# Attention scores drained two PSUM banks at a time, fewer value products in plain fp32, and the operand buffers of the out-projection placed earlier

## The chip, the cores and the metric

The kernel runs on one core of one Trainium2 chip. The metric is the device time of one execution in microseconds (us); the median of the runs is compared. A core has a matrix engine (PE, whose weight loads are listed as PEld), a vector engine (DVE), a scalar engine (ACT), a general engine (POOL) and a queue engine that issues transfers (SP). PE writes its results into PSUM, 8 banks of 512 fp32 columns for each of 128 partitions; the other engines read them from there.

## The reference

One block of a diffusion backbone over 2048 latent tokens of width 1024 with 256 context tokens: modulated norm, one input projection, gated linear attention (GLA, 4 heads) and differential softmax attention (4 heads, width 128) side by side, one output projection, and a modulated SwiGLU FFN. The part that the change is about:

```python
def diff_attend(q, k_all, v_all, lam):            # 2048 queries, 2304 keys, 2 maps of width 64
    s = jnp.einsum('bhqcd,bhkcd->bhcqk', qb, k_all) * (DIFF_DH ** -0.5)
    p = jax.nn.softmax(s, axis=-1)
    a = p[:, :, 0] - lam * p[:, :, 1]
    return jnp.einsum('bhqk,bhkd->bhqd', a, v_all)
...
mix = jnp.concatenate([gla_merge(...), diff_merge(...)], axis=-1) @ w_out[l]
x = x + gt1 * mix
```

Everything is fp32. Most products are made of three fp32r matmuls on operands split into a high and a low part; a plain fp32 matmul takes two passes on PE.

## The kernel before

The program has six stages one behind the other: projections (0 to some 400 us), the GLA scan (to 875), attention (scores from 875.6 to 1481.5, its last value products to 1516), the output projection (to 1751), and the two FFN products.

**Attention.** There are 16 blocks: 4 heads by 4 groups of 512 queries. A block has 4 query tiles of 128; each tile has two maps, and each map's scores over 2304 keys are made in 5 chunks (CH: four of 512 columns and one of 256), so a block has 8 maps and 40 chunks. For a chunk, two matmuls (L775, L776; the high and the low part of the queries) fill one PSUM bank `s`; one DVE instruction (L777) copies the bank into the row buffer p0 or p1 and takes its maximum into a column of `mx`. After the fifth chunk DVE reduces `mx` to `nm` (L781) and ACT makes the exponentials of the whole row with their sum (L783). Four chunks after the second map, `combine` weights the second map (r and cf, L799 and L801; p1 times cf in two halves, L807) and POOL adds the halves to p0 (L83).

**Value products.** The stream `av_stream` runs 12 chunks behind. A block has 18 key tiles. For each the step is: four transposes of p0 into a PSUM tile `t` (L820); a copy out of it; and, two steps later (LOOK), the product with that key tile's values. Key tiles with kt % 6 in VFP, (0, 3) before, stay fp32: one ACT copy `at` (L823) and one fp32 matmul (L843). The others are split: ACT writes the high part `ah` (L89), DVE the rest `al` (L86), and three fp32r matmuls follow (L92 to L94). In a block, a step follows the chunks 1, 4, 6, 8, 10, 12, 15, 17, 19, 21, 24, 26, 28, 30, 32, 35, 37 and 39 (counted from 0). At a block's end ACT copies the result (`ot`, L848), PE transposes it (L860), ACT copies it (`on`, L862), and SP stores it to `md` (L864).

**PSUM.** The score pool ps_s has NS = 4 tiles of one bank, ps_t 3, ps_o 1: all 8 banks.

**Order.** The order on PE is the order of the code (manual_schedule with MS = PE). On DVE, ACT, POOL and SP a scheduler orders by priorities, and each engine then runs its list strictly in that order.

**Values.** Stage 1 stores the values either as fp32 (key tiles in VF) or as high and low parts; `load_v` (L735 to L750) loads them per head and third of the keys.

**Output projection.** For each token tile `prep` loads `md` into mx (L976), takes the square sums on ACT (L985, which writes its unused squares into mh), the deviation (L990) and its inverse (L992), scales (L995), transposes (L1002) and makes mh and ml, the two parts of the operand (L1004 to L1007); `main` multiplies by w_out (L1010). The pools ph (mh, ml), htp and wp are opened one behind the other (L914 to L916), so their order sets which addresses of the finished attention they reuse.

Of the kernel before, what the change touches and what calls it, by code (L numbers as in the profile page):

```python
# [11 lines left out]
F32 = mybir.dt.float32  # L12
F32R = mybir.dt.float32r
AF = mybir.ActivationFunctionType
ALU = mybir.AluOpType
AX = mybir.AxisListType
PSUM = bass.MemoryType.PSUM
DRAM = bass.MemoryType.DRAM

P = 128  # L20
# [12 lines left out]
NS, NTB, NO = 4, 3, 1  # L33
# [6 lines left out]
CD, LAG, LOOK = 4, 12, 2  # L40
MS = {mybir.EngineType.PE}
BKL = (3, 6, 9, 12)
PB, VFP = 6, (0, 3)
CSPLIT = ((2, 0, 1152), (2, 1152, 2304))
WPOOL = (0,)
VF = tuple(t for t in range(NK // P) if t % 6 in VFP)
# [5 lines left out]
def dit_block(ctx: ExitStack, tc: tile.TileContext, x, c, cx, c_ctx, w_mod, b_mod, norm1_g, w_in, gate_up,  # L52
              gate_bias, gla_g, qn_g, kn_g, lam_q, lam_k, diff_g, w_out, norm2_g, w_fi, w_fo,
              cosf, sinf, lmask, out, dbg=None):
    nc = tc.nc
    V, S, T, G = nc.vector, nc.scalar, nc.tensor, nc.gpsimd
# [115 lines left out]
    with ExitStack() as st:  # L172
# [3 lines left out]
        st1 = st.enter_context(ExitStack())  # L176
# [12 lines left out]
        for t in range(2):  # L189
            xt = wk.tile([P, D], F32, name="xt", tag="xt")  # L190
# [514 lines left out]
    with ExitStack() as st:  # L705
        sm = st.enter_context(tc.tile_pool(name="s3m", bufs=6, reuse_waits="tile"))
# [4 lines left out]
        qp = st.enter_context(tc.tile_pool(name="s3q", bufs=2, reuse_waits="tile"))  # L711
        kp_ = st.enter_context(tc.tile_pool(name="s3k", bufs=3, reuse_waits="tile"))
        pb = st.enter_context(tc.tile_pool(name="s3pb", bufs=PB, reuse_waits="tile"))
        ps_s = st.enter_context(tc.tile_pool(name="s3ps", bufs=NS, space=PSUM, reuse_waits="tile"))
        ps_t = st.enter_context(tc.tile_pool(name="s3pt", bufs=NTB, space=PSUM, reuse_waits="tile"))
        ps_o = st.enter_context(tc.tile_pool(name="s3po", bufs=NO, space=PSUM, reuse_waits="tile"))
        NKT = NK // P
        CH = [(0, 512), (512, 512), (1024, 512), (1536, 512), (2048, 256)]
# [42 lines left out]
        def score_stream():  # L761
            later, ring = [], iter(range(64))
            for bi, (h, qb, i0, nq) in enumerate(blocks):
                as_[bi] = []
                for i in range(i0, i0 + nq):
                    qd = qs_[h, qb, i // 2]
                    qc = slice(i % 2 * P, (i % 2 + 1) * P)
                    pr = [(pa if next(ring) % (4 + PB) < 4 else pb).tile([P, NK], F32, name="p0", tag="p0"), sp.tile([P, NK], F32, name="p1", tag="p1")]
                    as_[bi].append(pr[0])
                    ls = []  # L770
                    for c_ in range(2):
                        mx = sm.tile([P, 5], F32, name="mx", tag="mx")
                        for j, (o0, n) in enumerate(CH):
                            ps = ps_s.tile([P, 512], F32, name="s", tag="s")
                            T.matmul(ps[:, 0:n], qd[0][c_][:, qc], ks_[h, c_][:, o0:o0 + n], start=True, stop=False)  # L775
                            T.matmul(ps[:, 0:n], qd[1][c_][:, qc], ks_[h, c_][:, o0:o0 + n], start=False, stop=True)  # L776
                            V.tensor_scalar(out=pr[c_][:, o0:o0 + n], in0=ps[:, 0:n], scalar1=1.0, scalar2=-3.0e38,  # L777
                                            op0=ALU.mult, op1=ALU.max, accum_out=mx[:, j:j + 1])
                            if j == len(CH) - 1:
                                nm = sm.tile([P, 1], F32, name="nm", tag="nm")  # L780
                                V.tensor_reduce(out=nm, in_=mx, axis=AX.X, op=ALU.max, negate=True)  # L781
                                l = l0all[:, qb * 4 + i, h:h + 1] if c_ == 0 else sm.tile([P, 1], F32, name="l1", tag="l1")
                                S.activation(pr[c_], pr[c_], AF.Exp, bias=nm, accum_out=l)  # L783
                                ls.append(l)
                                if c_ == 1:
                                    later.append([CD, combine(pr, ls, bi == len(blocks) - 1 and i >= i0 + nq - 2)])
                            for e in list(later):
                                e[0] -= 1
                                if e[0] < 0:
                                    e[1]()  # L790
                                    later.remove(e)
                            yield
            for e in later:
                e[1]()
# [72 lines left out]
        due, n = [], 0  # L867
# [26 lines left out]
    with ExitStack() as st:  # L894
# [16 lines left out]
        st1 = st.enter_context(ExitStack())  # L911
        xlp = rsk.enter_context(tc.tile_pool(name="s4xl", bufs=1, side="right", reuse_waits="tile"))
        gp = st1.enter_context(tc.tile_pool(name="s4gt", bufs=1, reuse_waits="tile"))
        htp = st1.enter_context(tc.tile_pool(name="s4ht", bufs=2, reuse_waits="tile"))  # L914
        wp = st1.enter_context(tc.tile_pool(name="s4w", bufs=1, reuse_waits="tile"))
        ph = st1.enter_context(tc.tile_pool(name="s4h", bufs=2, reuse_waits="tile"))  # L916
        ps_gm = st1.enter_context(tc.tile_pool(name="s4gm", bufs=1, space=PSUM, reuse_waits="tile"))
        ps_tp = st1.enter_context(tc.tile_pool(name="s4tp", bufs=3, space=PSUM, reuse_waits="tile"))
        ps_mm = st1.enter_context(tc.tile_pool(name="s4mm", bufs=4, space=PSUM, reuse_waits="tile"))
# [9 lines left out]
        state = {}  # L929
        wo = {k: tuple(wp.tile([P, D], F32R, name=f"wo{u}_{k}") for u in "hl") for k in ORD1}  # L930
        for n, k in enumerate(ORD0):
            pool, tag = {3: (xnp, "xn"), 2: (xnp, "xn"), 1: (ph, "mh"), 0: (ph, "ml")}.get(k, (xp, "xt"))
            w = pool.tile([P, D], F32, name="wr", tag=tag)
            load(w, w_out[0, k * P:(k + 1) * P, :])
            with tc.high_priority(offset=tc.cur_priority - marks[3 + 2 * n]):
                split(*wo[k], w)
# [316 lines left out]
        with tc.manual_schedule(engines=MS):  # L1253
# [6 lines left out]
            for m, (n, i) in enumerate(flat):  # L1260
# [13 lines left out]
                ps = product(n, i)  # L1274
# [104 lines left out]
```

## Time and profile before

| what | value |
|---|---|
| runs | 3092.88, 3094.99 and 3092.88 us, median 3092.88 |
| profiled execution | 3094.64 us, of which the span of the trace is 3092.9 |
| busy share over the span | PE 98%, PEld 80%, DVE 71%, ACT 46%, POOL 15% |
| granted clock of PE, mean | 0.992 of full speed |
| attention scores | 875.6 to 1481.5 us, a block each 38.2 us |

Read the shares with care: 98% of PE is a mean over stages, and the 71% of DVE too. In the attention stage both are nearly full, and there the rows below were read: how busy each engine is in stretches of 38 us (one block), who waits for whom, and the distance from one instruction's start to the next one's, which is what an instruction costs on a full engine (its own duration includes an overlap with its neighbour).

### The profile page before, as it was taken

The numbers are of one execution on the slowest core, as the hardware profiler recorded it, in microseconds if no ns is written. First come the engines' busy times: TensorE is split into PE (matmuls) and PEld (weight loads), VectorE is DVE, ScalarE is ACT, GpSimd is POOL, SyncE is SP. The second block draws the span as 40 slices with busy tenths as digits, with TensorE's granted clock in tenths as the row PEclk, the third lists the DMA queues.
The fourth block names the chain that finished last, engine by engine and source line by source line (L and its number), as shares of the span: only waits on it lengthen the run. The fifth ranks groups of instructions, "written<-read, shape, count | busy, mean of one in ns | idle before, by whom it ended". The sixth has DMA issues, their size and how long they took to land.

```text
span 3092.9 us, 41887 instructions
## 1 busy us (share of the span) xinstructions
PE 3016.1 (98%) x15124; PEld 2483.7 (80%) x15124; DVE 2203.8 (71%) x4788; ACT 1423.5 (46%) x2259; POOL 463.8 (15%) x290
## 2 busy tenths in 40 slices
PE   7999999999989999999999999999999999999999
PEld 4888888888867777777787788888788888888887
DVE  6887768888889999999787776666766666324232
ACT  5333366666657777777644433333433333113111
POOL 2111100000036555555111000000000000000000
PEclk9999999999999999999999999999999999999999
DMA  8876511121151313121445442222322225445342
GB/s 312 280 237 224 192 66 63 66 93 65 49 154 34 91 34 93 35 76 35 143 164 163 158 136 82 82 85 69 88 82 86 82 86 179 149 136 180 130 135 90
DMA packets 319121, 363.46 MB, mean 118 GB/s; under 512 B 25409, under 2 KB 256258, under 8 KB 312258
## 3 DMA queue, kind: packets, MB, share of 16 engines
q1 hardware_dynamic: 316322, 351.35, 36.2%
q0 software_dynamic: 2304, 8.39, 0.7%
q8 instruction: 119, 1.95, 0.3%
q10 hardware_dynamic: 288, 1.05, 0.1%
q14 instruction: 88, 0.72, 0.1%
HBM read 249.96 MB, written 110.76 MB: 117 GB/s over the span
## 4 chain that ended last, share of the span: by engine, by line
PE 63%; DVE 4%; issue 2%; DMA 1%; ACT 1%; POOL 1%; DVEq 0%; SPq 0%; ACTq 0%; POOLq 0%
PE p L93 9%; PE p L92 9%; PE p L94 9%; PE o L93 6%; PE o L94 6%; PE o L92 6%; PE s L775 4%; PE s L776 4%; PE t L820 4%; PE o L843 3%; PE mm L92 1%; PE mm L93 1%; PE mm L94 1%; POOL p L83 0%; DMA wo<-in_w_ffn_out 0%
## 5 line engine op out<-in xcount | busy, mean ns | idle before, releaser
L83 POOL TENSOR_TENSOR p<-p,p 128x1152 f32<-128x1152 f32 x124 | 354.8, 2882 | 283.5 <-DVE p L807 175.8
L777 DVE TENSOR_SCALAR_CACHE_REDUCE p<-s 128x512 f32<-128x512 f32 (+1 forms) x640 | 382.3, 632 | 13.2 <-PE s L776 9.2
L92 PE MATMUL mm<-wh,hh 128*128 128x512 f32 (+2 forms) x976 | 378.7, 388 | 0.0
L94 PE MATMUL mm<-wh,hl 128*128 128x512 f32 (+2 forms) x976 | 355.0, 364 | 1.1 <-DVE hl L86 1.1
L93 PE MATMUL mm<-wl,hh 128*128 128x512 f32 (+2 forms) x976 | 353.8, 363 | 0.0
L783 ACT ACTIVATE p<-p,nm 128x2304 f32<-128x2304 f32 x128 | 283.8, 2217 | 44.5 <-DVE nm L781 44.5
L775 PE MATMUL s<-k,qh 128*128 128x512 f32 (+1 forms) x640 | 276.4, 436 | 7.7 <-DVE p L777 6.9
L83 DVE TENSOR_TENSOR e<-p,e 128x512 f32<-128x512 f32 x220 | 152.1, 691 | 161.1 <-PE p L94 161.1
L92 PE MATMUL o<-wot,ah 128*128 128x512 f32 x682 | 265.4, 389 | 1.1 <-ACT wot L89 1.1
L93 PE MATMUL o<-wot,ah 128*128 128x512 f32 x682 | 265.4, 389 | 0.2 <-DVE wot L86 0.2
L94 PE MATMUL o<-wot,al 128*128 128x512 f32 x682 | 265.3, 389 | 0.0
L89 ACT ACTIVATE wh<-wi 128x512 fp32r<-128x512 f32 x172 | 108.4, 631 | 293.4 <-PE p L93 228.4
L776 PE MATMUL s<-k,ql 128*128 128x512 f32 (+1 forms) x640 | 235.6, 375 | 1.3 <-DMA ql<-ql 1.3
L89 ACT ACTIVATE ah<-ar 128x1408 fp32r<-128x1408 f32 x62 | 82.6, 1374 | 318.0 <-PE o L93 314.4
L94 PEld LDWEIGHTS mm<-wh,hl 128*128 128x128 f32 x976 | 184.8, 189 | 31.2 <-DVE hl L86 1.5
L92 PEld LDWEIGHTS mm<-wh,hh 128*128 128x128 f32 x976 | 185.9, 190 | 22.9 <-issue 0.7
L93 PEld LDWEIGHTS mm<-wl,hh 128*128 128x128 f32 x976 | 186.1, 191 | 21.4 <-issue 0.5
L86 DVE TENSOR_TENSOR al<-ar,ah 128x1408 fp32r<-128x1408 f32 x62 | 98.3, 1622 | 134.1 <-ACT ah L89 134.1
L89 ACT ACTIVATE wh<-s 128x512 fp32r<-128x512 f32 x128 | 80.9, 632 | 221.9 <-PE p L93 208.5
L820 PE MATMUL t<-ident,p 128*128 128x128 f32 x1152 | 173.3, 273 | 0.8 <-POOL p L83 0.8
L820 PEld LDWEIGHTS t<-ident,p 128*128 128x128 f32 x1152 | 141.5, 141 | 35.3 <-issue 3.7
L775 PEld LDWEIGHTS s<-k,qh 128*128 128x128 f32 x640 | 122.5, 191 | 57.9 <-DVE p L777 15.8
(317 smaller groups left out, 7135.9 us busy)
## 6 DMA issues: line engine op xcount, KB each, us to landing
ar<-act SPq DMA_DIRECT2D x64, 704.0 KB, 5.9
wi<-in_w_ffn_in SPq DMA_DIRECT2D x86, 512.0 KB, 5.0
act<-e SPq DMA_DIRECT2D x88, 256.0 KB, 2.6
wm<-in_w_mod SPq DMA_DIRECT2D x32, 512.0 KB, 5.0
xt<-in_x SPq DMA_DIRECT2D x30, 512.0 KB, 4.7
wr<-in_w_in SPq DMA_DIRECT2D x12, 1024.0 KB, 7.8
hdh<-hh SPq DMA_DIRECT2D x9, 1024.0 KB, 4.8
hdl<-hl SPq DMA_DIRECT2D x9, 1024.0 KB, 6.6
```

The costliest lines, as they stand in the source:

```text
L83: (eng or V).tensor_tensor(out=o, in0=a, in1=b, op=ALU.add)
L86: return (eng or V).tensor_tensor(out=o, in0=a, in1=b, op=ALU.subtract)
L89: return S.activation(hi, src, AF.Copy), sub(lo, src, f(hi))
L92: T.matmul(ps, a[0], b[0], start=start, stop=False, **how)
L93: T.matmul(ps, a[0], b[1], start=False, stop=False, **how)
L94: T.matmul(ps, a[1], b[0], start=False, stop=stop, **how)
L775: T.matmul(ps[:, 0:n], qd[0][c_][:, qc], ks_[h, c_][:, o0:o0 + n], start=True, stop=False)
L776: T.matmul(ps[:, 0:n], qd[1][c_][:, qc], ks_[h, c_][:, o0:o0 + n], start=False, stop=True)
L777: V.tensor_scalar(out=pr[c_][:, o0:o0 + n], in0=ps[:, 0:n], scalar1=1.0, scalar2=-3.0e38, op0=ALU.mult, op1=ALU.max, accum_out=mx[:, j:j + 1])
L783: S.activation(pr[c_], pr[c_], AF.Exp, bias=nm, accum_out=l)
L820: T.transpose(pt[:, i, :], as_[bi][i][:, kt * P:(kt + 1) * P], ident)
L843: T.matmul(po[:, 0:nq, :], v[0], at[0], start=kt == 0, stop=kt == NKT - 1)
```

## The change

1. The score pool has two tiles of two banks instead of four of one. Chunks 0 and 1 share a tile, chunks 2 and 3 too, chunk 4 has one alone. One DVE instruction drains a tile: 1024, 1024 and 256 columns per map, 3 instead of 5. A row's `mx` has 3 columns.
2. VFP is (0,): key tiles 0, 6 and 12 of a block stay fp32, and 3, 9 and 15 are split like the others. So 48 of the 96 fp32 steps become split ones. Stage 1 stores three key tiles more in two parts, and load_v's tiles hold 1, 5 and 5 key tiles instead of 2, 4 and 4.
3. The pool ph is opened ahead of htp and wp; two raw rows of w_out use the buffers of mx instead of mh and ml. At the new addresses mh lies over the buffers of the last `al`, `ot` and `on` of attention; ml and the weights move up.

```diff
-PB, VFP = 6, (0, 3)
+PB, VFP = 6, (0,)
...
-        ps_s = st.enter_context(tc.tile_pool(name="s3ps", bufs=NS, space=PSUM, reuse_waits="tile"))
+        ps_s = st.enter_context(tc.tile_pool(name="s3ps", bufs=NS // 2, space=PSUM, reuse_waits="tile"))
...
-                        mx = sm.tile([P, 5], F32, name="mx", tag="mx")
+                        mx = sm.tile([P, 3], F32, name="mx", tag="mx")
                         for j, (o0, n) in enumerate(CH):
-                            ps = ps_s.tile([P, 512], F32, name="s", tag="s")
+                            if j % 2 == 0:
+                                ps2 = ps_s.tile([P, 2, 512], F32, name="s", tag="s")
+                            ps = ps2[:, j % 2]
...
-                            V.tensor_scalar(out=pr[c_][:, o0:o0 + n], in0=ps[:, 0:n], scalar1=1.0, scalar2=-3.0e38,
-                                            op0=ALU.mult, op1=ALU.max, accum_out=mx[:, j:j + 1])
+                            if j % 2 or j == len(CH) - 1:
+                                a0 = j // 2 * 1024
+                                V.tensor_scalar(out=pr[c_][:, a0:o0 + n], in0=ps2.rearrange("p b n -> p (b n)")[:, 0:o0 + n - a0],
+                                                scalar1=1.0, scalar2=-3.0e38, op0=ALU.mult, op1=ALU.max,
+                                                accum_out=mx[:, j // 2:j // 2 + 1])
...
+        ph = st1.enter_context(tc.tile_pool(name="s4h", bufs=2, reuse_waits="tile"))
         htp = st1.enter_context(tc.tile_pool(name="s4ht", bufs=2, reuse_waits="tile"))
         wp = st1.enter_context(tc.tile_pool(name="s4w", bufs=1, reuse_waits="tile"))
-        ph = st1.enter_context(tc.tile_pool(name="s4h", bufs=2, reuse_waits="tile"))
...
-            pool, tag = {3: (xnp, "xn"), 2: (xnp, "xn"), 1: (ph, "mh"), 0: (ph, "ml")}.get(k, (xp, "xt"))
+            pool, tag = {3: (xnp, "xn"), 2: (xnp, "xn"), 1: (pp, "mx"), 0: (pp, "mx")}.get(k, (xp, "xt"))
```

**First place: PE at the border of two maps without a value step between them** (chunks 33 to 35 of a block; the numbers of the tiles `s` tell which tile a matmul fills). Before, PE runs from the end of a step into these rows:

```order
L94 MATMUL o_12522<-ah_12648,vl1_10931 128x512
L775 MATMUL s_12716<-k1_10676,qh0_12427 128x512
L776 MATMUL s_12716<-k1_10676,ql0_12429 128x512
L775 MATMUL s_12728<-k1_10676,qh0_12427 128x256
L776 MATMUL s_12728<-k1_10676,ql0_12429 128x256
L775 MATMUL s_12736<-k1_12262,qh1_12428 128x512
L776 MATMUL s_12736<-k1_12262,ql1_12430 128x512
L820 MATMUL t_12740<-ident_60,p0_11848 128x128
```

And of the changed kernel, at the same place:

```order
L94 MATMUL o_12344<-ah_12465,vl1_10822 128x512
L778 MATMUL s_12517<-k1_10578,qh0_12253 128x512
L779 MATMUL s_12517<-k1_10578,ql0_12255 128x512
L778 MATMUL s_12543<-k1_10578,qh0_12253 128x256
L779 MATMUL s_12543<-k1_10578,ql0_12255 128x256
L778 MATMUL s_12551<-k1_12096,qh1_12254 128x512
L779 MATMUL s_12551<-k1_12096,ql1_12256 128x512
L826 MATMUL t_12554<-ident_60,p0_11701 128x128
```

The order of the matmuls is the same; what moved is whose banks they fill. With two tiles in turn, s_12551 takes the banks of s_12517, the tile that PE filled last but one; before, s_12736 took the bank of the chunk four earlier.

**Second place: DVE at the same border.** Before, DVE has these rows:

```order
L86 TENSOR_TENSOR al_12694<-t_12688,ah_12693 128x512
L777 TENSOR_SCALAR p0_12669,mx_12671<-s_12698 128x512
L777 TENSOR_SCALAR p0_12669,mx_12671<-s_12702 128x512
L777 TENSOR_SCALAR p0_12669,mx_12671<-s_12716 128x512
L799 RECIPROCAL r1_12720<-l1_12667 128x1
L777 TENSOR_SCALAR p0_12669,mx_12671<-s_12728 128x256
L801 TENSOR_SCALAR cf_12722<-l0all_80,r1_12720,neglam_81 128x1
L781 TENSOR_REDUCE nm_12732<-mx_12671 128x1
L777 TENSOR_SCALAR p1_12670,mx_12735<-s_12736 128x512
L807 TENSOR_SCALAR p1_12558<-p1_12558,cf_12722 128x1152 x2
```

And of the changed kernel:

```order
L86 TENSOR_TENSOR al_12510<-t_12504,ah_12509 128x512
L782 TENSOR_SCALAR p0_12486,mx_12488<-s_12489 128x1024
L805 RECIPROCAL r1_12535<-l1_12484 128x1
L807 TENSOR_SCALAR cf_12537<-l0all_80,r1_12535,neglam_81 128x1
L813 TENSOR_SCALAR p1_12381<-p1_12381,cf_12537 128x1152
L86 TENSOR_TENSOR al_12526<-t_12520,ah_12525 128x512
L782 TENSOR_SCALAR p0_12486,mx_12488<-s_12517 128x1024
L813 TENSOR_SCALAR p1_12381<-p1_12381,cf_12537 128x1152
L782 TENSOR_SCALAR p0_12486,mx_12488<-s_12543 128x256
L787 TENSOR_REDUCE nm_12547<-mx_12488 128x1
```

Three drains of 512 became one and a half of 1024; one half of the combination and the `al` of a key tile that was fp32 before now stand between the drain of s_12489 and that of s_12517.

**Third place: ACT at the end of attention**, where prep of the first two token tiles begins (mx_16480 and mx_16169 are the rows of the first one; g_sd belongs to the norm of GLA's half). Before, its squares stand among the last copies of the value products:

```order
L823 ACTIVATE at_16248<-t_16243 128x512
L985 ACTIVATE mh_16512,ss4_16514<-mx_16480 128x128 x3
L89 ACTIVATE ah_16258<-t_16253 128x512
L985 ACTIVATE mh_16512,ss4_16514<-mx_16480 128x128
L89 ACTIVATE ah_16270<-t_16265 128x512
L990 ACT_TABLE_LOAD
```

In the changed kernel they stand behind the last copies of attention:

```order
L89 ACTIVATE ah_16021<-t_16016 128x512
L854 ACTIVATE ot_16034<-o_15843 128x512
L868 ACTIVATE on_16041<-t_16036 128x512
L968 ACTIVATE mx_16169<-kk_16181 128x512
L140 ACT_TABLE_LOAD
L140 ACTIVATE g_sd_16194<-gss_16192,eps_t_67 128x4
L991 ACTIVATE mh_16201,ss4_16203<-mx_16169 128x128 x4
L996 ACTIVATE sd4_16211<-ss4_16203 128x4
```

The squares (L985 before, L991 now) write mh, which now shares addresses with `on`; they moved behind `on`, and the program makes them wait for the four stores out of it.

## Rows read from the trace of the kernel before

**Rows 1.** Busy time by stretch: length, PE, PEld, DVE, ACT, POOL (instructions), PEclk, DMA, GB/s.
```profile
900.00:938.00 38.00, 33.75 (x142) 25.14 (x141) 33.67 (x111) 23.70 (x26) 25.45 (x9) 0.86 0.18 56
...
1432.00:1470.00 38.00, 38.00 (x203) 30.23 (x202) 36.84 (x116) 28.38 (x37) 22.89 (x8) 1.00 0.15 46
...
1490.00:1516.00 26.00, 24.20 (x132) 17.65 (x131) 22.24 (x36) 24.22 (x55) 1.29 (x1) 1.00 0.71 212
```

**Rows 2.** Waits from 1200 to 1460 us: total us, times, longest.
```profile
DVE p L777 <- PE s L776: 3.1, 14, 0.2
```

**Rows 3.** Timeline of ACT: the first and the fifteenth block end, start first.
```profile
959.27 0.60 ACT L848 ACTIVATE ot<-o 128x512 f32<-128x512 f32 x1
...
1494.24 0.60 ACT L848 ACTIVATE ot<-o 128x512 f32<-128x512 f32 x1
```

**Rows 4.** Timeline of DVE in one block: start, duration, instruction [idle before].
```profile
1208.53 0.41 DVE L777 TENSOR_SCALAR_CACHE_REDUCE p<-s 128x256 f32<-128x256 f32 x1
...
1208.86 0.27 DVE L801 TENSOR_SCALAR cf<-l0all,r,neglam 128x1 f32<-128x1 f32 x1
...
1209.11 0.68 DVE L777 TENSOR_SCALAR_CACHE_REDUCE p<-s 128x512 f32<-128x512 f32 x1
...
1209.72 1.55 DVE L807 TENSOR_SCALAR p<-p,cf 128x1152 f32<-128x1152 f32 x2
...
1211.18 0.68 DVE L86 TENSOR_TENSOR al<-t,ah 128x512 fp32r<-128x512 f32 x1
...
1211.78 0.68 DVE L777 TENSOR_SCALAR_CACHE_REDUCE p<-s 128x512 f32<-128x512 f32 x1
```

**Rows 5.** Timeline of PE in the same block.
```profile
1210.41 0.60 PE L820 MATMUL t<-ident,p 128*128 128x128 f32 x4
...
1212.16 0.28 PE L775 MATMUL s<-k,qh 128*128 128x256 f32 x1
...
1212.40 0.60 PE L820 MATMUL t<-ident,p 128*128 128x128 f32 x4
...
1213.53 0.39 PE L775 MATMUL s<-k,qh 128*128 128x512 f32 x1
...
1213.99 0.40 PE L775 MATMUL s<-k,qh 128*128 128x512 f32 x1
```

**Rows 6.** Timeline where one engine waited for another.
```profile
1477.10 0.28 PE L775 MATMUL s<-k,qh 128*128 128x256 f32 x1
...
1477.30 0.69 DVE L777 TENSOR_SCALAR_CACHE_REDUCE p<-s 128x512 f32<-128x512 f32 x1 [0.22 <-PE s L776]
...
897.98 0.09 DVE L777 DVE_READ_ACCUMULATOR p<-s 128x1 f32 x1
...
898.12 0.79 PE L775 MATMUL s<-k,qh 128*128 128x512 f32 x1 [1.33 <-DVE p L777]
...
1208.35 0.60 PE L820 MATMUL t<-ident,p 128*128 128x128 f32 x4
...
1209.05 0.60 ACT L89 ACTIVATE ah<-t 128x512 fp32r<-128x512 f32 x1 [0.35 <-PE t L820]
```

**Rows 7.** The end of attention: timeline, and the stores of `on` (durations, first and last).
```profile
1505.37 0.34 ACT L985 ACTIVATE mh<-mx 128x128 fp32r<-128x128 f32 x1
...
1514.48 1.28 ACT L995 ACTIVATE mx<-mx,rs 128x128 f32<-128x128 f32 x4
...
1522.78 0.78 PE L92 MATMUL mm<-woh,mh 128*128 128x512 f32 x1
...
L864 SPq DMA_DIRECT2D md<-on x64: 319/430/1202, 964.7 to 1519.5; - x64
...
DMA to landing us min/median/max: 1.6/1.6/3.4
```

**Rows 8.** Busy time by stretch, columns as in rows 1, the start of attention.
```profile
892.00:896.00 4.00, 2.53 (x9) 1.27 (x8) 2.61 (x14) 1.92 (x3) 1.74 (x1) 1.00 0.65 156
896.00:900.00 4.00, 2.61 (x7) 1.79 (x8) 4.00 (x12) 1.74 (x3) 3.13 (x2) 0.61 0.92 368
```

## The prediction

> **What bounds the kernel now.** The changed part is attention, 606 of 3092.9 us, so I read the busy times by stretches of 38 us there first. In a steady block PE is busy for all of 38.00 us at full clock and DVE for 36.84 [rows 1]. So PE is the bound, and DVE has 1.2 us of slack in a block. The waits say how these two full engines get along: DVE waited for scores 3.1 us in 260 [rows 2], and among the waits none of PE for a drain is of that size. With four banks PE may be four chunks ahead, and DVE's long instructions are absorbed by that queue. A block takes (1494.2 - 959.3)/14 = 38.2 us from the first block's end to the fifteenth's [rows 3]. Only the first block looks different: in the stretch 900 to 938 PE is busy for 33.75 of 38 and its clock is 0.86 [rows 1], because it stands waiting for DVE there.
>
> **Prices.** On a full engine an instruction costs the distance to the next start. DVE: 256 columns drained 0.33 us, 512 columns 0.61, both halves of the combination 1.46 (so 0.73 each), cf and nm 0.25 together, `al` 0.60 [rows 4]. PE: a chunk of 512 columns 0.46, one of 256 0.24, a split value step (12.40 to 13.53) 1.13; an fp32 one is what lies between 10.41 and 12.40 less the two chunks in it, 1.99 - 0.70 = 1.29 [rows 5]. Hand-offs: DVE starts 0.20 after the pitch of the last score matmul ends (the next matmul starts at 77.10, the drain at 77.30); PE restarts 0.14 after the drain's (97.98 to 98.12) [rows 6]. A drain of 1024 columns isn't in the trace. From 256 to 512 it grows by 0.28, so 0.61 + 2 x 0.28 = 1.17 (estimate); the bounds are 1.22, two drains of today, and 1.1, if a fixed part of 0.06 fell away twice.
>
> **The change in sums.** Merging saves 2 x 0.61 - 1.17 = 0.05 us for each of 16 merged drains, 0.8 us of DVE in a block. The three key tiles that are split now cost DVE 3 x 0.60 = 1.8 and spare PE 3 x (1.29 - 1.13) = 0.48; ACT copies a tile either way. So DVE goes from 37.0 (36.84 x 38.2/38) to 38.0 of 38.2 us, and PE from 38.2 to 37.7. If only sums counted, a block would get shorter by 0.2 to 0.5 us. [...]
>
> **What the sums leave out: two tiles in a ring.** Before, a chunk took the bank that had been filled four chunks earlier. Now the tiles alternate: chunks 0 and 1 of a map in A, 2 and 3 in B, 4 in A, and the next map's chunks 0 and 1 again in B. So PE can't begin a map until DVE has emptied the banks of chunks 2 and 3, which PE finished with only the short chunk 4 in between. That hand-off takes 0.20 + 1.17 + 0.14 = 1.51 us even if DVE starts at once. The cover is chunk 4 (0.24), and a value step (1.13) where one follows chunk 3 or 4. By the list of steps that is so at 6 of 8 maps of a block; behind the chunks 14 and 34 there is none. Least loss: 6 x (1.51 - 1.37) + 2 x (1.51 - 0.24) = 0.8 + 2.5 = 3.4 us in a block, against 0.48 gained. The other reuses (chunk 4 of chunks 0 and 1; chunks 2 and 3 of chunk 4) have two chunks and a step between, and cost nothing at the least.
>
> DVE doesn't start at once, though: it is full, and in its order other work stands ahead of the drain. Take the second place shown with the change, and count from the end of the last score of s_12489. PE makes a chunk (0.46), a value step (1.13), a chunk (0.46) and chunk 4 (0.24): free at 2.29. DVE drains s_12489 from 0.20 to 1.37, then r and cf (0.25) to 1.62, half a combination (0.73) to 2.35, and al_12526 (0.60) to 2.95; that tile's `ah` is no later (its transposes began at 0.46, ACT starts 0.70 behind them and takes 0.60 [rows 6]: 1.76). Only then does it drain s_12517, to 4.12, and PE begins s_12551 at 4.26, 2.0 us late. Before, s_12736 took a bank long emptied.
>
> I walked one whole block like this, row by row along the changed order of PE and DVE with these prices, carrying the lateness over. The stalls are 2.4 (this place, where DVE comes late already), 1.5, 1.2, 0.9 and four smaller ones, 7.1 us together, against the least of 3.4. PE's own work is 0.5 shorter, so a block takes 6.6 us more. While PE stands DVE catches up; when PE fills the two banks, DVE runs dry: neither is full any more. I count 15 blocks, as the first waits for DVE already: 15 x 6.6 = **+99 us**.
>
> **The other edits.** The squares of prep: before, they lay between the copies of the last value products. Now mh lies over `on`, whose last store is issued at 1519.5 and lands 1.6 later and more: some 1521.5 [rows 7]. Behind that come four squares (0.34 each by duration, 1.4), four scales (1.28), and deviation, inverse, transposes and copies, for which I allow 1.8, an estimate from six instructions of about the 0.3 of a square: main could begin at 1526, against 1522.78 [rows 7]. The wait heads ACT's queue, and the scaling and operands of the first token tiles stand behind it. On the other hand ACT is the fullest engine from 1490 to 1516 (24.22 of 26, PE 24.20 [rows 1]) and loses several us of work there, worth up to 1.8. I take **+3**, with bounds of 0 and +7. Stage 1 gets three key tiles to split and three stores more, for DVE, ACT and SP that have other work beside PE: I take 0, up to +2. Loading 5 split tiles per third instead of 4 lies under whole blocks: 0.
>
> **Sum.** 3094.6 (the profiled execution) + 99 + 3 = 3196.6; the median lies 1.8 lower than that execution: **3195 us**.
>
> **Rivals.**
> (1) *Only the least hand-off.* If the chip's DVE gets to chunks 2 and 3 at once, as its list would allow where PE's lateness gives it time to clear the rest, a block loses 3.4 - 0.5 = 2.9: 16 x 2.9 = 46, so 3094.6 + 46 + 3 - 1.8 = 3142. For it: DVE's sum (38.0) is far under the 44.8 us of my block, so it has slack. Against it: its order is fixed, and the example has 1.6 us of other work ahead of the drain.
> (2) *The clock falls as well.* Between 892 and 900 PE is busy for 2.53 and 2.61 of each 4 us while it waits for DVE, and in the second of these stretches the granted clock is 0.61 [rows 8]; the whole stretch to 938 has 0.86 [rows 1]. In my walk PE is busy for 84% of a block, with 2.4 us idle at one place. At 0.86, 37.4 us of PE work take 6.1 more; half of that lies under waits that are there anyway: 16 x 3 = 48 on top, 3243. For it: the idle places return in each block. Against it: in the steady part the idle time is cut by value steps, unlike at 892. [...]
> (3) *Not slower.* If PE never finds a tile undrained, because DVE takes chunks 2 and 3 within the 0.24 or 1.37 us of cover, the sums hold: -0.2 to -0.5 a block, 3094.6 - 1.8 - 3 to 8 = 3085 to 3090, with up to 3 of the transition back. It decides where a drain of 1024 columns takes under about 1.0 us and is first in DVE's list; both would have to be so, and the drain alone speaks against it.
> (4) *The change doesn't do what it says*: if drained tiles were released bank by bank, PE could start on the first bank earlier. But the release is one semaphore of one instruction, so I count this in (1).
>
> **How the numbers follow.** Chances: forecast 0.52, (1) 0.18, (2) 0.20, (3) 0.10. The range reaches from (1) with a cheap transition and a drain of 1.1, 3135, to (2), 3245; outside lie (3) and the worst of (2). A difference under 0.2% (6 us) can't be told from none here. Case (3) is half faster and half the same; all the others are slower: 0.05, 0.05, 0.90.
>
> **What the profile would show.** The forecast is right if PE is busy for about 84% of a block and the waits list the first score matmul behind the drain with some 7 us a block, the longest 2 to 2.4, with `ot` copies 44 to 45 us apart at a clock of 1.00. If they are 41 apart, (1) holds; if the clock of the blocks is under 0.95, (2). If a 1024 drain's distance is not near 1.17, the hand-off is mis-sized by that difference, 8 times a block. The squares should start behind the landing of the stores, near 5.5 us after the last value product. The forecast falls if DVE's idle time in a block stays near zero, as then the sums set the end.

## The result and the profile after

The changed kernel takes 3219.86 us in the median of 4 runs (3214.85 to 3220.62), the kernel before 3093.93 (3092.88 to 3096.36): a ratio of 1.0402, 95% interval 1.0384 to 1.042, so 4% slower. The forecast was 3195 us, in a range of 3135 to 3245. The profiled execution has a span of 3218.8 us against 3092.9, 125.9 more. By the starts of the first and last matmul of each stage:

| stretch | before | after | difference |
|---|---|---|---|
| up to the first score matmul | 875.6 | 877.8 | +2.2 |
| to the last value matmul (1515.73; 1639.74) | 640.1 | 761.9 | +121.8 |
| to the first matmul of the out-projection (1522.78; 1649.99) | 7.05 | 10.25 | +3.2 |
| from there to the end of the span | 1570.1 | 1568.8 | -1.3 |

So 97% of the loss is in attention. The 2.2 us ahead of it and the 1.3 behind lie within the scatter between executions: the traces of all runs below, with the change in stage 1 or without it, begin the scores between 873.4 and 879.1 us, and from the first matmul of the out-projection they take 1566.7 to 1576.7 us. In attention the stretches of one block each (busy time by stretch, columns as in rows 1) read:

```profile
1035.60:1082.75 47.15, 41.66 (x209) 32.25 (x208) 40.22 (x88) 28.75 (x36) 22.40 (x8) 0.96 0.39 95
1082.75:1129.80 47.05, 41.54 (x209) 32.18 (x207) 40.12 (x87) 28.87 (x36) 22.39 (x8) 0.96 0.20 58
1129.80:1175.30 45.50, 40.00 (x209) 30.97 (x207) 40.04 (x87) 28.75 (x36) 22.41 (x8) 1.00 0.10 30
```

Against [rows 1], where PE filled all of 38.00 us and DVE 36.84, neither engine is full: PE idles 5.5 us in each of them and DVE 5.5 to 7. Two lengths occur, 45.5 at a granted clock of 1.00 and 47.1 at 0.96; of thirteen distances between block ends in the middle eight are the longer one. The waits from 1200 to 1460 us (total us, times, longest) name the cause; compare [rows 2]:

```profile
PEld s L778 <- DVE p L782: 48.0, 50, 2.6
PE s L778 <- DVE p L782: 31.4, 23, 2.4
DVE p L782 <- PE s L779: 18.8, 29, 1.6
```

Each engine waits for the other now: PE for the drain of scores, and DVE for scores, 18.8 us in place of 3.1. Where PE stands in the block that begins at 1129.80 shows in its timeline (idle time and its cause in brackets), with three rows of DVE around the first of these idles:

```profile
1132.42 0.50 PE L778 MATMUL s<-k,qh 128*128 128x512 f32 x1 [2.42 <-DVE p L782]
1148.73 0.50 PE L778 MATMUL s<-k,qh 128*128 128x512 f32 x1 [1.24 <-DVE p L782]
1154.49 0.50 PE L778 MATMUL s<-k,qh 128*128 128x512 f32 x1 [1.14 <-DVE p L782]
1170.74 0.50 PE L778 MATMUL s<-k,qh 128*128 128x512 f32 x1 [0.64 <-DVE p L782]
...
1130.54 0.68 DVE L86 TENSOR_TENSOR al<-t,ah 128x512 fp32r<-128x512 f32 x1
1131.14 1.22 DVE L782 TENSOR_SCALAR_CACHE_REDUCE p<-s 128x1024 f32<-128x1024 f32 x1
...
1132.28 1.76 DVE L813 TENSOR_SCALAR p<-p,cf 128x1152 f32<-128x1152 f32 x1
```

The 2.42 is the place worked out in the prediction: half a combination (its row, at 1129.81, is in the last section) and `al` stand ahead of the drain of chunks 2 and 3 on DVE, the drain goes from 1131.14 to 1132.28, and PE starts 0.14 later. Four idles give 5.44 us; smaller waits hide in the modelled ends of matmuls and show on the weight loads (PEld), which wait 48.0 us where PE's own rows say 31.4.

### The profile page after: what moved, and what is told of

It is laid out like the page before. It is cut to its first block, busy times and chain, and to the rows that moved or that the text cites. A ratio compares the mean times of both kernels' runs of the same rounds, so it can differ in the third digit from the quotient of the medians.

```text
span 3218.8 us, 41518 instructions
## 1 busy us (share of the span) xinstructions
PE 3052.5 (95%) x15172; PEld 2503.2 (78%) x15172; DVE 2248.1 (70%) x4327; ACT 1423.3 (44%) x2259; POOL 460.1 (14%) x290
## 4 chain that ended last, share of the span: by engine, by line
PE 56%; DVE 13%; ACT 4%; issue 3%; DMA 1%; SPq 0%; POOL 0%; DVEq 0%; ACTq 0%; POOLq 0%
PE p L94 8%; PE p L93 8%; PE p L92 8%; PE o L93 6%; PE o L94 6%; PE o L92 6%; DVE p L782 5%; PE s L778 3%; PE t L826 3%; PE s L779 2%; ACT p L789 2%; DVE p L813 2%; DVE al L86 1%; PE mm L92 1%; PE mm L93 1%
## 5 line engine op out<-in xcount | busy, mean ns | idle before, releaser
L83 POOL TENSOR_TENSOR p<-p,p 128x1152 f32<-128x1152 f32 x124 | 347.5, 2818 | 405.1 <-DVE p L813 389.8
L782 DVE TENSOR_SCALAR_CACHE_REDUCE p<-s 128x1024 f32<-128x1024 f32 (+1 forms) x384 | 361.8, 951 | 59.2 <-PE s L779 58.9
L89 ACT ACTIVATE ah<-t 128x512 fp32r<-128x512 f32 x240 | 138.3, 590 | 212.4 <-PE t L826 212.2
L86 DVE TENSOR_TENSOR al<-t,ah 128x512 fp32r<-128x512 f32 x240 | 164.1, 686 | 31.8 <-ACT ah L89 29.6
```

The costliest lines, as they stand in the source:

```text
L83: (eng or V).tensor_tensor(out=o, in0=a, in1=b, op=ALU.add)
L86: return (eng or V).tensor_tensor(out=o, in0=a, in1=b, op=ALU.subtract)
L89: return S.activation(hi, src, AF.Copy), sub(lo, src, f(hi))
L782: V.tensor_scalar(out=pr[c_][:, a0:o0 + n], in0=ps2.rearrange("p b n -> p (b n)")[:, 0:o0 + n - a0], scalar1=1.0, scalar2=-3.0e38, op0=ALU ...
```

## The experiments

All times are medians of the runs, and a ratio is to the kernel before; "a block" is the distance of two `ot` copies in the middle of attention in the trace, 38.49 us in the kernel before.

**One part at a time.** First the drains alone (the run e_two). The edit is that of the change in the score stream; the other two parts are as before, so against the changed kernel:

```diff
-PB, VFP = 6, (0,)
+PB, VFP = 6, (0, 3)
...
-        ph = st1.enter_context(tc.tile_pool(name="s4h", bufs=2, reuse_waits="tile"))
         htp = st1.enter_context(tc.tile_pool(name="s4ht", bufs=2, reuse_waits="tile"))
         wp = st1.enter_context(tc.tile_pool(name="s4w", bufs=1, reuse_waits="tile"))
+        ph = st1.enter_context(tc.tile_pool(name="s4h", bufs=2, reuse_waits="tile"))
...
-            pool, tag = {3: (xnp, "xn"), 2: (xnp, "xn"), 1: (pp, "mx"), 0: (pp, "mx")}.get(k, (xp, "xt"))
+            pool, tag = {3: (xnp, "xn"), 2: (xnp, "xn"), 1: (ph, "mh"), 0: (ph, "ml")}.get(k, (xp, "xt"))
```

> The kernel before with the score pool of two two-bank tiles and the drains of 1024 alone (values and out-projection buffers as before). Theory (hand-off of two tiles in a ring): PE's work is 38.2 us in a block and DVE's falls to some 36.2, yet the first score matmul of a map still waits for the drain of the map before; nearly the whole loss is here, 44 to 46 us a block, 3175 to 3210 us. Rival (DVE overfilled by the third split key tile): without that tile DVE has 2 us of slack in a block, so the time is that of before within 10 us.

Measured: 3211.56 against 3095.06, ratio 1.0381 (1.0363 to 1.04), a block of 46.25 us. The stretch from 1200 to 1290, with the columns of before:

```profile
1200.00:1290.00 90.00, 80.51 (x398) 60.14 (x396) 76.56 (x166) 56.04 (x69) 44.68 (x16) 0.98 0.28 71
```

DVE has 13.4 us of 90 to spare and PE 9.5: the loss needs no overfilled DVE. The rival falls; this part alone makes 117 of the 126 us, a little above the top of what was expected. The clock isn't the cause here: it is 0.96 in six of thirteen blocks and 1.00 in the others, and all thirteen are 46.2 to 46.4 us long.

Then the value steps alone (the run e_split), with four one-bank tiles:

```diff
-PB, VFP = 6, (0, 3)
+PB, VFP = 6, (0,)
```

> The kernel before with one fp32 key tile in six alone (four one-bank tiles, out-projection buffers as before). Theory: four banks hide DVE; DVE's sum becomes 37.0 + 1.8 = 38.8 us a block against PE's 37.7, so DVE sets the pace, + 0.6 a block, 3095 to 3110 us. Rival (overfilled DVE makes the loss of the whole change): 3180 us and more.

Measured: 3113.52, ratio 1.0058 (1.0043 to 1.0073), a block of 39.24 us. From 1200 to 1390:

```profile
1200.00:1390.00 190.00, 189.24 (x1003) 150.88 (x1002) 188.86 (x578) 138.81 (x174) 112.25 (x40) 1.00 0.22 59
```

Here DVE is busy 99.4% of the time and sets the pace, as its sum of 38.8 said; block and time came out a little above the expected range. So this part alone is a loss too, of 18 us: it spares the full PE and loads the engine that was nearly as full. 117 + 18 is more than the whole change lost; a likely reason, not tested by itself, is that DVE has room for the third `al` where the hand-off holds PE up (13.4 us of 90 free in the run e_two).

Last, the buffers of the out-projection alone (the run e_ph):

```diff
+        ph = st1.enter_context(tc.tile_pool(name="s4h", bufs=2, reuse_waits="tile"))
         htp = st1.enter_context(tc.tile_pool(name="s4ht", bufs=2, reuse_waits="tile"))
         wp = st1.enter_context(tc.tile_pool(name="s4w", bufs=1, reuse_waits="tile"))
-        ph = st1.enter_context(tc.tile_pool(name="s4h", bufs=2, reuse_waits="tile"))
...
-            pool, tag = {3: (xnp, "xn"), 2: (xnp, "xn"), 1: (ph, "mh"), 0: (ph, "ml")}.get(k, (xp, "xt"))
+            pool, tag = {3: (xnp, "xn"), 2: (xnp, "xn"), 1: (pp, "mx"), 0: (pp, "mx")}.get(k, (xp, "xt"))
```

> The kernel before with the buffers of mh and ml opened first and the raw rows of w_out in mx alone. Theory: attention is as before; from the last value product to the first matmul of the out-projection 10.3 us in place of 7.05, as in the changed kernel, so 3 us more: 3094 to 3100 us. Rival: the squares that leave ACT's list at the end of attention give it back there, difference under 1 us.

Measured: 3096.6 against 3095.06, ratio 1.0005 (0.9996 to 1.0015). The timeline of this kernel shows the step as forecast: ACT waits for the stores of `on`, and PE for the scaled rows.

```profile
1521.59 0.31 ACT L985 ACTIVATE mh<-mx 128x128 fp32r<-128x128 f32 x1 [1.04 <-DMA md<-on]
...
1524.00 2.21 PE L1002 MATMUL tp<-ident,mx 128*128 128x128 f32 x8 [6.21 <-ACT mx L995]
```

The first matmul of the out-projection starts at 1526.1, 3.3 us later than the 1522.78 of [rows 7]; 0.3 of that lies ahead of attention (scores from 875.9 against 875.6), so 3.0 are the transition's. Whether it reaches the end can't be told: the interval is -1 to +5 us.

**A ring of three (the run e_ring3).** Chunk 4 gets a one-bank tile of its own, so that chunks 0 and 1 always use the same two banks, and chunks 2 and 3 the other two. Its bank comes from the transposes, which keep two of their three tiles.

```diff
-NS, NTB, NO = 4, 3, 1
+NS, NTB, NO = 4, 2, 1
...
-                                ps2 = ps_s.tile([P, 2, 512], F32, name="s", tag="s")
+                                if j < len(CH) - 1:
+                                    ps2 = ps_s.tile([P, 2, 512], F32, name="s", tag="s")
+                                else:
+                                    ps2 = ps_s.tile([P, 1, 512], F32, name="s1", tag="s1", bufs=1)
```

> The changed kernel with a third tile in the ring: chunk 4 has a one-bank tile of its own, so chunks 0 and 1 use the same banks in each map, chunks 2 and 3 too; the bank is taken from the transposes (2 tiles t, not 3). Theory: a map begins in banks that were filled a whole map earlier, less than 0.5 us a block is lost there; a block takes 38 to 39 us, 3090 to 3115 us, more only if two tiles t are too few. Rival (the long drain itself holds things up, wherever the tiles lie): 44 us a block and more, 3180 us and up.

Measured: 3143.51, ratio 1.0158 (1.0141 to 1.0175), a block of 40.85 us. This lies between both expectations, so the price of the lost tile t was measured by itself, in the kernel before (the run e_ntb2):

```diff
-NS, NTB, NO = 4, 3, 1
+NS, NTB, NO = 4, 2, 1
```

> The kernel before with two tiles t for the transposes in place of three, nothing else: what the bank taken in the run e_ring3 costs by itself. Theory (what was left of the loss there, 40.85 us a block against 38.5, is the missing tile t): a block of 39.5 to 41 us, 3110 to 3140 us. Rival (two tiles t are enough, and the long drain costs it): 3090 to 3100 us.

Measured: 3111.68, ratio 1.0057 (1.0042 to 1.0072), a block of 39.46 us: 1.0 us a block of the 2.4 that the ring of three lost. For the rest, the waits of the ring of three from 1200 to 1380 us:

```profile
PE t L869 <- DVE al L86: 5.7, 5, 1.1
...
PEld s L781 <- DVE p L785: 3.0, 8, 0.5
```

PE's wait for drains has gone from PE's rows; weight loads wait 3.0 us for them in 180, where the changed kernel had 48.0 in 260. What PE waits for now is a tile t, held by `al`, once a block (1.1 us). So the hand-off theory holds for the wait that it names, though some 1.4 us a block are left that these rows do not show. If the wait for `al` were the rest, fewer split tiles would help (the run e_ring3v):

```diff
-PB, VFP = 6, (0,)
+PB, VFP = 6, (0, 3)
```

> The run e_ring3 with two fp32 key tiles in six. Theory: what the ring of three lost (40.85 us a block) is the missing tile t, whose tiles wait for the al of DVE where a key tile is split; with fewer split tiles 39.5 us as in the run e_ntb2, 3105 to 3125 us. Rival (the drains of 1024 hold it up): 40.8 us a block and more, 3140 us and up.

Measured: 3159.2, ratio 1.0208 (1.0193 to 1.0223), a block of 41.76 us: slower, not faster. The time lies in the rival's range, but the rival's reason, the drains, isn't in the waits. The lines of PE from 1200 to 1390 (busy columns, then idle before and its cause) show what stands there:

```profile
L829 PE MATMUL t<-ident,p 128*128 128x128 f32 x324 | 49.0, 274 | 4.1 <-ACT at L832 3.6
L781 PE MATMUL s<-k,qh 128*128 128x256 f32 x36 | 10.6, 295 | 0.8 <-DVE p L785 0.8
L869 PE MATMUL t<-ident,ot 128*128 128x128 f32 x16 | 2.9, 310 | 4.6 <-DVE al L86 4.6
```

The drains cost 0.8 us in 190. The transposes wait for a tile t held by `al` (4.6) as before, and now also for one held by `at` (3.6). These waits are 2 us of the 3.3 that a block is longer than 38.49; the rest is in idles too short for the modelled ends, and stays open.

**Cover for the hand-off (the run e_step).** The steps are placed so that one stands between chunks 2 and 3 and the next map at every border:

```diff
-            due += [n + LAG + kt * 10 * blk[3] / NKT for kt in range(NKT)]
+            due += [n + k for k in (13, 16, 18, 21, 23, 26, 28, 29, 31, 33, 36, 38, 41, 43, 46, 48, 49, 51)]
```

> The changed kernel with the value steps placed behind the chunks 1 and 3 of each map, and two more behind chunk 4 of the sixth and the second map, so that a step of 1.13 us stands between chunks 2, 3 and the next map at every border. Theory: the two borders without cover go, 2.5 us of least loss in a block, 16 x 2.5 = 40 us: 3160 to 3200 us. Rival (DVE's queue and not the missing cover sets the wait): within 10 us of 3220.

Measured: 3153.43, ratio 1.0192 (1.0175 to 1.0209), a block of 42.05 us at a clock of 1.00: a little below the expected range. 66 us of the 126 go by moving value steps, 26 more than the two uncovered borders were to give. The clock's dips go with them (1.6 us in eight blocks, some 13 us), and the two borders held more than the least of 2.5 us: their idles in the rows above are 2.42 (behind chunk 34) and 1.14 (behind chunk 14), 1.0 us a block more. One idle of 1.24 us a block is left. PE's line from 1200 to 1390, to be set beside the one of the changed kernel for the same 190 us (22.9 us of idle):

```profile
L778 PE MATMUL s<-k,qh 128*128 128x512 f32 x145 | 64.0, 441 | 5.2 <-DVE p L782 5.0
```

**DVE's order (the run e_lead).** The drains get a higher priority, so that they stand further ahead in DVE's list:

```diff
-                                V.tensor_scalar(out=pr[c_][:, a0:o0 + n], in0=ps2.rearrange("p b n -> p (b n)")[:, 0:o0 + n - a0],
+                                with tc.high_priority(offset=300):
+                                    V.tensor_scalar(out=pr[c_][:, a0:o0 + n], in0=ps2.rearrange("p b n -> p (b n)")[:, 0:o0 + n - a0],
...
```

> The changed kernel with the drains of scores moved forward in DVE's list (a higher priority for them; the same instructions). Theory (the hand-off of 1.5 us can't be covered, and what stands ahead of the drain on DVE adds to it): the second part goes, the first stays; a block falls from 46.5 us towards the least of 38.5 - 0.5 + 3.4 = 41.4, so 3135 to 3185 us. Rival (the order on DVE does not matter, the ring alone costs all 8 us): within 10 us of 3220. Rival (a drain that starts at once hides the ring): under 3110 us.

Measured: 3257.89, ratio 1.0529 (1.0513 to 1.0545), a block of 47.6 us, five of thirteen longer at a lower clock: outside all three. The waits from 1200 to 1390 us:

```profile
PE o L93 <- DVE al L86: 19.8, 8, 3.0
...
PE s L778 <- DVE p L783: 11.5, 11, 1.5
```

The wait for drains fell to 11.5 us in 190, but `al` came late, and PE waits 19.8 us for that. So what was moved ahead in this list was paid by what stands behind it; moving the drains ahead by this much did not come near the least of 41.4 us a block, and other distances weren't tried.

What stands ahead of the drain can be changed in another way too: both halves of the combination in one DVE instruction (the run e_whole).

```diff
+                if not last:
+                    V.tensor_scalar(out=pr[1], in0=pr[1], scalar1=cf, scalar2=None, op0=ALU.mult)
                 for e, o0, o1 in CSPLIT:
...
                     else:
-                        V.tensor_scalar(out=p1, in0=p1, scalar1=cf, scalar2=None, op0=ALU.mult)
                         add(p0, p1, p0, G)
```

> The changed kernel with both halves of the combination in one DVE instruction of 2304 columns ahead of POOL's two additions. In the changed kernel one second half in each block takes 1.76 us, not 0.82, where POOL is in the first half's addition. Theory (that 0.94 us lies on the path once a block): up to 15 us less, 3205 to 3216 us. Rival (it lies under the wait for scores): within 4 us of 3220. Later additions on POOL could also make it slower: above 3224 us.

Measured: 3236.46, ratio 1.0458 (1.0441 to 1.0476), a block of 47.8 us: slower, as the third case has it. In this kernel's timeline of PE, and of DVE just before:

```profile
1228.10 1.42 DVE L809 TENSOR_SCALAR p<-p,cf 128x2304 f32<-128x2304 f32 x1
...
1229.43 0.68 DVE L86 TENSOR_TENSOR al<-t,ah 128x512 fp32r<-128x512 f32 x1
...
1231.31 0.74 PE L778 MATMUL s<-k,qh 128*128 128x512 f32 x1 [3.04 <-DVE p L782]
```

The whole, 1.33 us from its start to that of the next, now stands ahead of the drain in place of a half of 0.73, and the idle behind it grows from 2.42 to 3.04: 0.62 us for 0.60 more. That is the hand-off theory's second part, shown in one place. The clock has a share in the time as well. It is 0.96 in all thirteen blocks here, such as this one, against eight of thirteen in the changed kernel:

```profile
1209.27:1257.05 47.78, 41.67 (x208) 32.23 (x207) 38.56 (x84) 28.99 (x37) 21.09 (x9) 0.96 0.33 78
```

Five dips more, at 1.6 us, are about 8 of the 17 us; the rest is some 0.7 us a block. Whether POOL's later additions cost anything, and what the 1.76 us of the second half cost in the changed kernel, isn't settled by this run.

**The clock (the run e_fill).** At the two borders without a value step, the matmuls of chunk 4 are made five times; each pass begins anew, so only time is added.

```diff
-                            T.matmul(ps[:, 0:n], qd[0][c_][:, qc], ks_[h, c_][:, o0:o0 + n], start=True, stop=False)
-                            T.matmul(ps[:, 0:n], qd[1][c_][:, qc], ks_[h, c_][:, o0:o0 + n], start=False, stop=True)
+                            for _ in range(5 if j == 4 and c_ == 0 and i % 2 == 1 else 1):
+                                T.matmul(ps[:, 0:n], qd[0][c_][:, qc], ks_[h, c_][:, o0:o0 + n], start=True, stop=False)
+                                T.matmul(ps[:, 0:n], qd[1][c_][:, qc], ks_[h, c_][:, o0:o0 + n], start=False, stop=True)
```

> The changed kernel with the two matmuls of chunk 4 repeated four times more at the borders behind the chunks 14 and 34 of each block (useless work of 8 x 0.12 = 0.95 us in a place where PE stands for 1.5 to 2.4 us anyway). Theory (the clock's dips come from PE's standing there): blocks of 47.1 us at a mean clock of 0.96 become blocks of 45.5 at 1.00, 10 x 1.6 = 16 us less, 3200 to 3208 us. Rival (the dips have another cause, or 0.95 us of filling is too little): 3215 to 3235 us with the clock as it was.

Measured: 3204.61, ratio 1.0358 (1.0342 to 1.0373), as the theory said; the blocks in the middle are 45.5 us each but one of 45.8. From 1200 to 1390 (busy time by stretch) the clock is full, and in the timeline of PE the idle at the border that had 2.42 is 1.46 (that of 1.14, at the other border, is gone):

```profile
1200.00:1390.00 190.00, 175.68 (x937) 138.09 (x936) 167.32 (x366) 120.97 (x152) 90.68 (x34) 1.00 0.21 55
```

```profile
1217.03 0.50 PE L779 MATMUL s<-k,qh 128*128 128x512 f32 x1 [1.46 <-DVE p L783]
```

15 us are won by useless work on the engine that was the bound. In the traces 12.6 of them are won in attention, which is what eight dips of 1.6 us are worth; the scores also begin 3.5 us earlier in this trace, within the scatter. So in this kernel the dips come from PE's standing there: eight blocks of thirteen have one in the changed kernel, none with 0.95 us of that idle filled.

**Another hand-off (the run e_hyb).** One two-bank tile for chunks 0 and 1, two one-bank tiles for the others. Against the kernel before:

```diff
-                            ps = ps_s.tile([P, 512], F32, name="s", tag="s")
+
+                            if j == 0:
+                                ps2 = ps_s.tile([P, 2, 512], F32, name="s", tag="s", bufs=1)
+                            elif j > 1:
+                                ps2 = ps_s.tile([P, 1, 512], F32, name="s1", tag="s1", bufs=2)
+                            ps = ps2[:, j if j < 2 else 0]
...
-                            V.tensor_scalar(out=pr[c_][:, o0:o0 + n], in0=ps[:, 0:n], scalar1=1.0, scalar2=-3.0e38,
-                                            op0=ALU.mult, op1=ALU.max, accum_out=mx[:, j:j + 1])
+                            if j:
+                                a0 = o0 if j > 1 else 0
...
```

> The kernel before with one two-bank tile for chunks 0 and 1 (one drain of 1024) and two one-bank tiles for chunks 2, 3 and 4; values, transposes and out-projection buffers as before. The hand-off that is tight now is another one: chunk 4 takes the bank of chunk 2, 0.20 + 0.61 + 0.14 = 0.95 us, covered by chunk 3 (0.46) and a value step at six of eight maps, not at the first and fifth. Theory (the loss is counted by tight hand-offs without cover): 2 x 0.49 = 1.0 us a block at least, 39.5 us a block, 3100 to 3125 us. Rival (a drain of two banks harms as such): half as many long drains as in the run e_two, half its loss, some 3150 us.

Measured: 3142.68, ratio 1.016 (1.0145 to 1.0175), a block of 41.5 us. The place is the expected one, the size isn't. PE's lines from 1200 to 1390 have a wait for drains on one form only, the first matmul of chunk 4:

```profile
L780 PE MATMUL s<-k,qh 128*128 128x256 f32 x37 | 13.4, 362 | 7.7 <-DVE p L784 7.7
```

But it waited 19 times in 4.6 blocks, four times a block and not at two maps of eight, and a block lost 3.0 us, not 1.0. The least takes DVE as free; here chunk 2's drain stands behind the drain of 1024, which can't begin before chunk 1 is done:

```profile
1213.73 1.22 DVE L784 TENSOR_SCALAR_CACHE_REDUCE p<-s 128x1024 f32<-128x1024 f32 x1
...
1214.87 0.69 DVE L784 TENSOR_SCALAR_CACHE_REDUCE p<-s 128x512 f32<-128x512 f32 x1
...
1215.62 0.39 PE L780 MATMUL s<-k,qh 128*128 128x256 f32 x1 [0.45 <-DVE p L784]
```

The time is near the rival's 3150; what argues against a harm of long drains as such is the place of the wait, not the sum. With one fp32 key tile in six (the run e_hybs):

> The same with one fp32 key tile in six. Theory: PE 0.5 us a block less, DVE 1.8 more and 8 x 0.06 less by the merged drains, some 38.7; with the tight hand-off 39 to 40 us a block, 3095 to 3125 us, and less than the run e_split (3113.5) if the merged drains help a full DVE at all. Rival: DVE's fuller list makes the tight hand-off later, over 3125 us.

Measured: 3162.82, ratio 1.0224 (1.0209 to 1.0239), 42.57 us a block: the time is the rival's, that a fuller DVE list makes the tight hand-off later, and it isn't less than that of the run e_split. No run beat the kernel before.

## Why the prediction was right

The direction, the place and the mechanism held, and the time lay in the range, 25 us above the forecast; some 23 of these are in attention. By its own steps:

- **The hand-off in a ring of two** was the loss: the drains alone lose 117 us, a third tile takes the wait for drains from PE's rows, and value steps placed at every border halve the loss. The worked border had 2.0 us at the least and 2.4 in the walk; the trace has 2.42. The other idles were to be 1.5, 1.2 and 0.9; they are 1.24, 1.14 and 0.64, with smaller ones on the weight loads.
- **Prices.** The unseen drain of 1024 took 1.14 us from start to start (1131.14 to 1132.28), 1.17 was taken; so a merged drain saved 0.08 us, for 0.05. PE restarts 0.14 behind it, as forecast. One half of the combination in each block took 1.76 us in place of 0.82 by duration (last section), which the walk did not have; it comes behind the drain at the worked border, and what it cost stays open.
- **The block.** Forecast were 44.8 us, measured are 45.5 at full clock. 0.3 of this is the base, the 38.2 that stands in the table of the kernel before too: [rows 3] reach to the fifteenth block, which ends after the scores do (34.56 us); the thirteen distances before it are 38.49, not 38.2. Against the right base the loss is 7.0, for 6.6.
- **The clock** was set as a rival with its whole price or none. It came in eight blocks of thirteen with 1.6 us each, some 13 us (12.6 by the traces of the run e_fill), and is about half of what the forecast missed. The walk had an idle of 2.4 us in each block, and [rows 8] a clock of 0.61 where PE waits for DVE: a reason to put part of that price in the sum.
- **The count of blocks.** The first was left out since it waits in the kernel before already [rows 1]; its end came 11.9 us later all the same, 2.2 of them from before the scores. So attention lost 121.8 us, not 99: some 10 up to the first `ot` copy, and 8.0 in each of the next fourteen distances.
- **The transition**: +3 taken, 3.2 measured, behind the landing of the stores as said. **Stage 1**: 0 was taken, up to +2. The 2.2 in the trace say nothing on it: other kernels with the same stage 1 begin the scores between 873.4 and 876.5 us, some earlier than the 875.6 of the kernel before.
- **Value steps**: in sums they were a gain of 0.2 to 0.5 us a block if queues hid the rest. The run e_split, without the merged drains, shows 0.75 lost, as DVE's sum, not PE's, sets the end with four banks. What the sums would give with merged drains as well, rival (3), no run shows, since the hand-off is in all that have them.

## What to carry to other kernels

Before two buffers are merged into a bigger one, count how far the producer may run ahead in the new ring, and set the whole turn (start delay, drain, restart) against the work that stands between two uses of the same buffer; the time saved by merging (0.08 us a drain here) is small beside one uncovered turn (1.5 us). Then look at what stands ahead of the drain in the consumer's strict list: it added to the turn one for one at the place measured here (0.62 us for 0.60 in the run e_whole), and moving the drain ahead only moved the wait (19.8 us in 190 for `al` in the run e_lead). Where two engines are both 97% full or more, as in the steady blocks here, taking work from one and giving more to the other can make the second the bound: in the run e_split DVE was busy 99.4% of the time, and a block took 39.24 us for 38.49.

## What the runs showed of the hardware

A DVE instruction of 1152 columns that took 0.82 us everywhere in the kernel before took 1.76 in the changed one, once a block, at the place where POOL was in its addition on the other half. The rows of the changed kernel:

```profile
1129.81 0.82 DVE L813 TENSOR_SCALAR p<-p,cf 128x1152 f32<-128x1152 f32 x1
1130.80 2.62 POOL L83 TENSOR_TENSOR p<-p,p 128x1152 f32<-128x1152 f32 x1 [2.80 <-DVE p L813]
```

POOL's row ends at 1133.42, and the DVE instruction that started at 1132.28 (shown in the result) ends at 1134.04, 0.62 us after. In the run e_two the same instruction starts earlier in POOL's addition, takes longer, and again ends 0.62 us behind it:

```profile
1131.13 2.63 POOL L83 TENSOR_TENSOR p<-p,p 128x1152 f32<-128x1152 f32 x1 [3.45 <-DVE p L813]
...
1132.02 2.36 DVE L813 TENSOR_SCALAR p<-p,cf 128x1152 f32<-128x1152 f32 x1
```

In both runs the DVE instruction is done 0.62 us behind POOL's, though it started 1.48 us into the addition in the changed kernel and 0.89 us into it in the run e_two. What couples the two, the rows do not show. Not every DVE instruction was held up: `al` at 1130.54 and the drain at 1131.14 overlapped POOL's addition and took their usual 0.68 and 1.22 us. Where both halves stand next to each other, in the kernel before and in the run e_step, no combination instruction was over 0.83 us (the longest are 0.82).

In the changed kernel the clock fell behind the idle of 2.4 us in eight of thirteen blocks and not in the other five, which have the same order and the same idle. Two stretches of 2 us, behind the idles that ended at 1085.36 and at 1132.42 (the third number from the end is the granted clock; in the first stretch the two matmuls of a chunk start 0.43 us apart, at 1088.43 and 1088.86, in the second 0.24, at 1134.13 and 1134.37):

```profile
1088.00:1090.00 2.00, 2.00 (x9) 1.59 (x8) 1.34 (x3) 1.86 (x2) 1.73 (x1) 0.54 0.04 8
1134.00:1136.00 2.00, 2.00 (x13) 1.61 (x12) 1.97 (x6) 1.68 (x2) 1.88 (x1) 1.00 0.00 0
```

With 0.95 us of added matmuls at each of the two borders (the run e_fill) no block dipped. With an idle of 3.04 us all thirteen did in the run e_whole, but with one of 3.0 us only five in the run e_lead. A long idle isn't needed either: the kernel of the moved steps, with an idle of 1.24 us in each block, kept a clock of 1.00, while in the run e_ring3v it fell in two of thirteen blocks, with none over 1.2 us:

```profile
1346.95 0.95 PE L869 MATMUL t<-ident,ot 128*128 128x128 f32 x4 [1.15 <-DVE al L86]
1348.00:1352.00 4.00, 4.00 (x15) 3.08 (x15) 1.69 (x8) 3.44 (x4) 0.00 (x0) 0.68 0.29 82
```

So the length of the idle alone doesn't tell where the clock falls, and no run here shows what does. What the run e_fill shows is that the dips ended with less idle time at the two borders (1.46 us in place of 2.42 at the one, and the 1.14 at the other gone). What a dip costs differs too: 1.6 us a block in the changed kernel, and nothing that can be seen in the run e_two, where all blocks are 46.2 to 46.4 us long.
